# Gathered expert rows in pairs: two rows per VectorE operation, with row sums and scalings on ScalarE

## The chip, the cores and the metric

One core of a Trainium2 chip runs the kernel in one launch. The metric is the device time of that launch in microseconds (us), the median of several executions; lower is better. PE is TensorE (the matmul engine), DVE is VectorE, ACT is ScalarE, POOL is GpSimd and SP is SyncE, which here only issues DMAs.

## The reference, cut to what matters

A decoder layer on 1024 tokens of width 1024. Its first part (a gated MLP beside a state-space model, with projections) is not touched by the change. The second part is a PEER feed-forward layer: each token gets 8 heads x 16 retrieved experts, each expert being one row of a table `u` and one row of a table `v` (16384 rows of 1024 float32 each), and then a last RMS norm:

```
idx, g = top 16 of 256 product-key candidates per head, softmax over them
act = gelu(einsum('thkd,td->thk', u_tab[idx], t))
w   = g * act
y   = einsum('thk,thkd->td', w, v_tab[idx])
x   = x + gt2 * y
return _rmsnorm(x, g_final)
```

For one token that is 128 dot products with rows of `u`, and a sum of 128 rows of `v` with weights.

## The kernel before, in words

The 1024 tokens are 8 blocks of 128, and a token stands on a partition. After about 900 us the scores and choices exist and the feed-forward layer starts, in which the blocks are treated in two ways at the same time.

*Dense blocks.* For five blocks (640 tokens) all 16384 experts are computed by matmul, as 128 tiles `i` of 128 experts. `stage1` (L917 to L931) forms the products `pa` of tile `i` in 2 x 24 matmuls of 128x320, and ACT puts a gelu on each half (L929). `weigh` (L941 to L951) multiplies by the choice weights `Gt` (DVE, L946, two halves), ACT casts the result to the high part `wh` (L949) and DVE forms the low part `wl` (L950). `load_u` and `load_v` (L902 to L915) fetch a tile's tables on SP's queue, ACT casts the high part (L905, L913), DVE the low part (L906, L914). After every four tiles (a group, 32 in all) `stage2` (L955 to L1006) multiplies by the rows of `v` in 10 units of 12 matmuls of 128x512: two blocks add up in PSUM (`res`, L964), for three blocks the result `pd` (L973) is added to `acc` by DVE (L981). `load_g` (L933 to L939) fetches the weights `Gt` of a group as two tiles in three buffers, by DMAs issued on ACT's queue.

*Gathered blocks.* For the other three blocks only the chosen rows are fetched. The generator `side_work` (L858 to L890) does it row by row. For each of 128 rows of `u`: POOL issues an indirect DMA of 128x1024 float32 into a slot `ru` of a ring of 6 (tag "row", 4 KB a partition each, L871), and one DVE instruction multiplies it with the block's tokens `hn` and adds up along the row into a column of `act` (L874, followed by a small instruction that reads the accumulator). Then gelu and the weights, and for each of 128 rows of `v` another gather into the ring (`rv`, L882) and one DVE instruction `gacc = rv * act + gacc` (L887; L885 for the first). At the end `finish` (L830 to L844) multiplies by `gt2` (L834), adds `x1` (`xf`, loaded by a DMA on POOL's queue, L850), takes the RMS norm (L836 on ACT, small operations of DVE, L843) and stores. The two constant rows `gt2` and `g_final` are fetched once for the whole loop into tiles of their own (`final_rows`, L853 to L856).

The main loop (end of the listing) goes through the 128 tiles and after each pulls six rows of the side work. A scheduler then sets one static order per engine; each engine takes its instructions strictly in that order. At the end the remaining side work is pulled (`pull(10 ** 9)`), and the last `stage2` finishes the five dense blocks: it loads `x1` on POOL's queue, multiplies `acc` by `gt2` (L999) and adds (L1000), and each finished `pd` or `res` goes through L834, L835, L836 and L843 of `finish`.

## Time and profile before

| | us |
|---|---|
| median of 3 executions | 2688.28 |
| the three | 2693.47, 2676.6, 2688.28 |
| span of the profiled execution | 2681.3 |
| the part ahead of the loop (not touched) | about 913 |
| loop with the side work, 913 to about 2622 | about 1709 |
| from the last `pa` matmul to the end | about 59 |

The profile is of one execution, and its engine times are shares of its span of 2681.3 us, which lies 7.0 us under the median and inside the three executions. A busy share is an average over the whole span; what matters for a change in the loop is read from the loop's own stretches, and there from who waits for whom. "Idle before" is time an engine stood before an instruction, with the instruction or DMA that ended the wait.

### The profile page before, as it was taken

What the parts mean: (1) busy time and instruction counts of PE and PEld (TensorE: products, weight loads), DVE (VectorE), ACT (ScalarE), POOL (GpSimd) and SP (SyncE); (2) the same over time, 40 slices, a digit from 0 to 9 for tenths busy, and PEclk for the clock granted to TensorE, in tenths of its full rate; (3) what the DMA queues carried; (4) which work ended last, traced back from release to release, by engine and by line L of the source; (5) the groups of instructions that cost most, each with busy time, mean ns of one, the idle gap of its engine ahead of it and who ended that gap; (6) DMA issues with size and microseconds to landing.
All of it is one profiled execution on the core that took longest, in us unless ns stands there. A gap on an engine that the chain in (4) does not pass through costs nothing.

```text
span 2681.3 us, 39165 instructions
## 1 busy us (share of the span) xinstructions
PE 2549.5 (95%) x14119; PEld 2171.5 (81%) x14119; DVE 2302.3 (86%) x5013; ACT 903.2 (34%) x1612; POOL 1038.4 (39%) x842
## 2 busy tenths in 40 slices
PE   6999999999878999999999999999999999999995
PEld 2557676588667898999889999888998899998894
DVE  7984699869899888888898988789897889888998
ACT  2311246578877422222222222222222222222222
POOL 0001000000000255566665665556565456555662
PEclk9996999999997999999999999999999999999998
DMA  9646232342545699999999999989999899998995
GB/s 351 114 151 181 101 134 103 111 157 111 200 139 198 236 348 316 324 330 330 330 359 342 344 332 324 331 312 345 335 341 333 301 330 368 336 332 305 353 322 201
DMA packets 298115, 724.76 MB, mean 270 GB/s; under 512 B 42384, under 2 KB 133008, under 8 KB 292384
## 3 DMA queue, kind: packets, MB, share of 16 engines
q0 software_dynamic: 112832, 411.09, 41.9%
q1 hardware_dynamic: 88800, 254.48, 26.6%
q10 hardware_dynamic: 96288, 56.69, 7.5%
q8 instruction: 111, 1.82, 0.3%
q14 instruction: 84, 0.69, 0.1%
HBM read 658.60 MB, written 62.39 MB: 269 GB/s over the span
## 4 chain that ended last, share of the span: by engine, by line
PE 24%; issue 23%; DVE 21%; POOL 15%; DMA 10%; ACT 5%; POOLq 0%; ACTq 0%; DVEq 0%
POOL rv L882 12%; PE pa L927 6%; DVE jk L874 4%; DMA Gt<-G_d 4%; PE pd L973 4%; POOL ru L871 3%; ACT b L687 3%; PE res L964 3%; PE pq L724 2%; PE po L626 2%; PE pgs L689 2%; DMA ru<-in_peer_u_dram,ix 1%; ACT GS L692 1%; PE pzs L360 1%; DMA vr<-in_peer_v_dram 1%
## 5 line engine op out<-in xcount | busy, mean ns | idle before, releaser
L927 PE MATMUL pa<-Th,u 128*128 128x320 f32 x4096 | 912.4, 310 | 8.7 <-DVE acc L981 5.3
L871 POOL DMA_INDIRECT ru<-in_peer_u_dram,ix x384 | 503.2, 1310 | 1016.4 <-issue 702.0
L927 PEld LDWEIGHTS pa<-Th,u 128*128 128x128 f32 x4096 | 688.3, 188 | 13.5 <-issue 3.3
L882 POOL DMA_INDIRECT rv<-in_peer_v_dram,ix x384 | 515.0, 1341 | 341.7 <-DVE gacc L887 271.1
L927 PE MATMUL pa<-Tl,u 128*128 128x320 f32 x2048 | 634.3, 310 | 0.0
L973 PE MATMUL pd<-v,wh 128*128 128x512 f32 x1536 | 482.4, 392 | 17.0 <-ACT v L913 6.9
L887 DVE SCALAR_TENSOR_TENSOR gacc<-rv,act,gacc 128x1024 f32<-128x1024 f32 x381 | 487.7, 1280 | 8.0 <-DMA rv<-in_peer_v_dram,ix 5.1
L874 DVE CUSTOM_DVE_ANT_0 jk<-ru,hn 128x1024 bf16<-128x1024 f32 x384 | 468.0, 1219 | 14.0 <-DMA ru<-in_peer_u_dram,ix 10.8
L927 PEld LDWEIGHTS pa<-Tl,u 128*128 128x128 f32 x2048 | 385.8, 188 | 1.2
L973 PEld LDWEIGHTS pd<-v,wh 128*128 128x128 f32 x1536 | 288.3, 189 | 81.8 <-ACT v L913 10.7
L964 PE MATMUL res<-v,wh 128*128 128x512 f32 x1024 | 319.4, 390 | 0.8 <-ACT wh L949 0.8
L973 PE MATMUL pd<-v,wl 128*128 128x512 f32 x768 | 299.9, 391 | 0.2 <-DVE wl L950 0.2
L946 DVE TENSOR_TENSOR w<-w,Gt 128x320 f32<-128x320 f32 x256 | 123.6, 483 | 184.7 <-DMA Gt<-G_d 181.4
L905 ACT CAST u<-ur 128x1024 fp32r<-128x1024 f32 x128 | 134.4, 1050 | 429.2 <-PE pd L973 231.1
L949 ACT CAST wh<-w 128x640 fp32r<-128x640 f32 x128 | 93.1, 728 | 492.7 <-DVE w L946 492.4
L687 ACT ACTIVATE b<-hot,gT 128x128 f32<-128x128 f16 x520 | 233.0, 536 | 59.5 <-PE pgs L689 40.2
L689 PE MATMUL pgs<-a,b 128*128 128x128 f32 x1280 | 191.0, 302 | 43.3 <-DVE a L679 21.0
L689 PEld LDWEIGHTS pgs<-a,b 128*128 128x128 f32 x1280 | 172.5, 210 | 65.2 <-ACT b L687 32.7
L964 PEld LDWEIGHTS res<-v,wh 128*128 128x128 f32 x1024 | 192.1, 188 | 40.7 <-ACT wh L949 1.2
L929 ACT ACTIVATE w<-pa 128x320 f32<-128x320 f32 x256 | 109.5, 434 | 281.5 <-PE pa L927 228.3
L964 PE MATMUL res<-v,wl 128*128 128x512 f32 x512 | 199.2, 390 | 1.4 <-DVE wl L950 1.4
L973 PEld LDWEIGHTS pd<-v,wl 128*128 128x128 f32 x768 | 144.8, 188 | 31.0 <-DVE wl L950 0.6
(348 smaller groups left out, 2994.5 us busy)
## 6 DMA issues: line engine op xcount, KB each, us to landing
vr<-in_peer_v_dram SPq DMA_DIRECT2D x128, 512.0 KB, 7.1
ur<-in_peer_ut_dram SPq DMA_DIRECT2D x128, 512.0 KB, 7.1
G_d<-GS SPq DMA_DIRECT2D x40, 1024.0 KB, 5.9
Gt<-G_d ACTq DMA_DIRECT2D x64, 640.0 KB, 16.4
wada<-in_w_ada_dram SPq DMA_DIRECT2D x17, 1024.0 KB, 13.3
wo<-in_w_out_dram SPq DMA_DIRECT2D x8, 1024.0 KB, 4.9
ru<-in_peer_u_dram,ix POOLq DMA_INDIRECT x384, 7.2
rv<-in_peer_v_dram,ix POOLq DMA_INDIRECT x384, 7.3
```

The costliest lines, as they stand in the source:

```text
L687: A.activation(b1[:, n], hot[:, :, o + n], AF.Copy, scale=gT[:, s1 + o + n:s1 + o + n + 1])
L689: T.matmul(pg[:, o // 4, (o % 4) * P:(o % 4 + 1) * P], b1[:, o % 2], a1[:, o % 4], start=True, stop=True)
L871: G.indirect_dma_start(out=row, out_offset=None, in_=a["peer_u"], in_offset=bass.IndirectOffsetOnAxis(ap=ix[:, s:s + 1], axis=0))
L874: V.tensor_tensor_reduce(out=junk, in0=row, in1=hn, scale=1.0, scalar=0.0, op0=ALU.mult, op1=ALU.add, accum_out=act[:, s:s + 1])
L882: G.indirect_dma_start(out=row, out_offset=None, in_=a["peer_v"], in_offset=bass.IndirectOffsetOnAxis(ap=ix[:, s:s + 1], axis=0))
L887: V.scalar_tensor_tensor(ac, row, act[:, s:s + 1], ac, op0=ALU.mult, op1=ALU.add)
L905: A.copy(u[:, 0], ur)
L927: T.matmul(pa[:, :NN], l[:, k, :], r[:, k, ns], start=(k == 0 and m == 0), stop=(k == KD - 1 and m == 2))
L929: A.activation(w[:, ns], pa[:, :NN], AF.Gelu_apprx_tanh)
L946: V.tensor_mul(w3, w3, Gt[i // QG][n][:, :, q * 32:(q + 1) * 32])
L964: T.matmul(res[tb][:, n, :], l[:, ts], r[:, n * 512:(n + 1) * 512], start=(g == 0 and q == 0 and m == 0), stop=(g == NGR - 1 and q == QG - ...
L973: T.matmul(po, l[:, ts], r[:, n * 512:(n + 1) * 512], start=(q == 0 and m == 0), stop=(q == QG - 1 and m == 2))
```

## The change

The gathered rows are handled in pairs (`GP = 2`). A ring slot holds two rows, and there are 4 slots (8 rows, 8 KB a partition and slot) in place of 6 of one row. `fetch` issues the two gathers of a pair one behind the other.

For `u`, DVE multiplies the pair in place by the tokens in one plain multiplication of 128x2048, and ACT sums each row by an activation with `accum_out`. For `v`, ACT scales each row in place by its weight (the first pair into the sum), and DVE adds the pair to a sum of two rows in one addition of 128x2048; at the block's end the two halves of the sum are added. The rows `gt2` and `g_final` are no longer kept: each block fetches them at its end into a slot of the ring, by two DMAs on ACT's queue; the `x1` tile takes a ring slot too, as it did before. The order of pulls is the same (six rows per tile), and ahead of the loop each engine's order is the same as before.

```
-            for s in range(NS):
-                row = rp.tile([P, D], F32, tag="row", name=f"ru{n}_{s}")
-                G.indirect_dma_start(out=row, ...)
-                junk = rp.tile([P, D], BF16, tag="junk", name=f"jk{n}_{s}", bufs=1)
-                V.tensor_tensor_reduce(out=junk, in0=row, in1=hn, scale=1.0, scalar=0.0, op0=ALU.mult,
-                                       op1=ALU.add, accum_out=act[:, s:s + 1])
-                yield
+            def fetch(src, s0, name):
+                row = rp.tile([P, GP, D], F32, tag="row", name=f"{name}{n}_{s0}")
+                for e in range(GP):
+                    G.indirect_dma_start(out=row[:, e], out_offset=None, in_=a[src],
+                                         in_offset=bass.IndirectOffsetOnAxis(ap=ix[:, s0 + e:s0 + e + 1], axis=0))
+                return row
+
+            for s in range(0, NS, GP):
+                row = fetch("peer_u", s, "ru")
+                V.tensor_mul(row, row, bcast(hn, 1, GP))
+                for e in range(GP):
+                    A.activation(junk, row[:, e], AF.Copy, accum_out=act[:, s + e:s + e + 1])
+                    yield
...
-                    V.scalar_tensor_tensor(ac, row, act[:, s:s + 1], ac, op0=ALU.mult, op1=ALU.add)
...
+            ac2 = rp.tile([P, GP, D], F32, tag="hn", name=f"gacc{n}", bufs=1)
+            for s in range(0, NS, GP):
+                row = fetch("peer_v", s, "rv")
+                for e in range(GP):
+                    A.activation(row[:, e] if s else ac2[:, e], row[:, e], AF.Copy, scale=act[:, s + e:s + e + 1])
+                    yield
+                if s:
+                    V.tensor_add(ac2, ac2, row)
+            ac = ac2[:, 0]
+            V.tensor_add(ac, ac, ac2[:, 1])
+            final_rows(rp, n)
+            x1 = load_x1(NDB + n, rp.tile([P, GP, D], F32, tag="row", name=f"xf{n}")[:, 0])
```

The static order changes only in the loop. DVE near the end, before: the weights of the last two tiles (`w`, `wl`), with the rows `rv_113` and later of the last gathered block between and behind them (line numbers of the kernel before).

```order
L950 TENSOR_TENSOR wl_22826<-w_22770,wh_22825 128x640
L946 TENSOR_TENSOR w_22852<-w_22852,Gt_0_22518 128x320
L887 SCALAR_TENSOR_TENSOR gacc_20995<-rv_116_22982,act_18351,gacc_20995 128x1024
L946 TENSOR_TENSOR w_22852<-w_22852,Gt_1_22520 128x320
L950 TENSOR_TENSOR wl_22908<-w_22852,wh_22907 128x640
L887 SCALAR_TENSOR_TENSOR gacc_20995<-rv_119_22991,act_18351,gacc_20995 128x1024
L834 TENSOR_TENSOR res_7531<-res_7531,fin_7698 128x512
L834 TENSOR_TENSOR pd_2_0_23160<-pd_2_0_23160,fin_7698 128x512
L1000 TENSOR_TENSOR x_1_23043<-x_1_23043,acc 128x1024
L887 SCALAR_TENSOR_TENSOR gacc_20995<-rv_127_23015,act_18351,gacc_20995 128x1024
L834 TENSOR_TENSOR pd_2_1_23173<-pd_2_1_23173,fin_7698 128x512
L1000 TENSOR_TENSOR x_1_23043<-x_1_23043,acc 128x1024
```

DVE near the end in the changed kernel, from the last additions of pairs (`rv_126` is the last pair; L894 there is the addition, L896 that of the halves, L955 and L959 what L946 and L950 were, L1008 what L999 was).

```order
L894 TENSOR_TENSOR gacc_20616<-gacc_20616,rv_124_22626 128x2048
L990 TENSOR_TENSOR acc<-acc,pd_4_1_22283 128x512
L915 TENSOR_TENSOR u_22357<-ur_22355,u_22357 128x1024
L894 TENSOR_TENSOR gacc_20616<-gacc_20616,rv_126_22632 128x2048
L1008 TENSOR_TENSOR acc<-acc,fin_22639 128x1024 x3
L955 TENSOR_TENSOR w_22302<-w_22302,Gt_0_22137 128x320
L896 TENSOR_TENSOR gacc_20616<-gacc_20616 128x1024
L955 TENSOR_TENSOR w_22302<-w_22302,Gt_1_22139 128x320
L835 TENSOR_TENSOR gacc_20616<-gacc_20616,fin_22639 128x1024
L959 TENSOR_TENSOR wl_22363<-w_22302,wh_22362 128x640
L836 TENSOR_TENSOR xf_22642<-xf_22642,gacc_20616 128x1024
```

The last gathered row thus moves from behind the last tile's weights, among the final multiplications, to ahead of the weights of the third tile from the end, and its `finish` stands among the last tiles.

ACT's queue around the issue of a group's second `Gt` tile, before (L929 the gelus, L949 `wh`, L938 the issue).

```order
L929 ACTIVATE w_10925<-pa_0_10926 128x320
L938 DMA Gt_1_11072<-G_d 128x10x128
L929 ACTIVATE w_10925<-pa_1_10952 128x320
L905 CAST u_10980<-ur_10978 128x1024
L949 CAST wh_10985<-w_10925 128x640
L938 DMA Gt_0_11554<-G_d 128x10x128
L929 ACTIVATE w_11012<-pa_0_11013 128x320
L913 CAST v_10991<-vr_10989 128x1024
L929 ACTIVATE w_11012<-pa_1_11039 128x320
L949 CAST wh_11076<-w_11012 128x640
```

The same place of the changed kernel, in a stretch where rows of `v` are scaled (L891; L938 are the gelus there, L947 the issue, L958 `wh`).

```order
L938 ACTIVATE w_11276<-pa_0_11277 128x320
L891 ACTIVATE rv_58_11358<-rv_58_11358,act_7700 128x1024
L938 ACTIVATE w_11276<-pa_1_11303 128x320
L891 ACTIVATE rv_60_11432<-rv_60_11432,act_7700 128x1024
L947 DMA Gt_1_11423<-G_d 128x10x128
L891 ACTIVATE rv_60_11432<-rv_60_11432,act_7700 128x1024
L958 CAST wh_11336<-w_11276 128x640
L947 DMA Gt_0_11905<-G_d 128x10x128
L891 ACTIVATE rv_62_11438<-rv_62_11438,act_7700 128x1024
L938 ACTIVATE w_11363<-pa_0_11364 128x320
L891 ACTIVATE rv_62_11438<-rv_62_11438,act_7700 128x1024
```

The issue of `Gt_1` now stands behind the second gelu and two rows' scalings, where it stood right behind the first gelu.

## Rows read from the trace of the kernel before

**Rows 1.** Windows of the loop (913 to 1531 and 1531 to 2601 us) and of the end; the columns are the stretch, its length, the busy time of PE, PEld, DVE, ACT and POOL with their instructions, the granted clock of PE as a share of full speed, the DMA share and GB/s.

```profile
913.00:1531.00 618.00, 614.51 (x3449) 560.08 (x3448) 539.15 (x718) 159.23 (x228) 370.21 (x278) 1.00 0.94 337
1531.00:2601.00 1070.00, 1058.28 (x5928) 962.85 (x5927) 930.11 (x1226) 265.49 (x385) 625.73 (x476) 1.00 0.92 332
...
2640.00:2681.30 41.30, 15.58 (x56) 11.95 (x54) 36.20 (x117) 8.05 (x22) 1.79 (x4) 0.73 0.46 178
```

**Rows 2.** The chain of waits in the loop: start, length and what, for the first pieces of three groups.

```profile
916.48 28.16 PE pa L927 x192
...
1475.64 28.16 PE pa L927 x192
...
1531.02 7.05 PE pa L927 x48
```

**Rows 3.** PE's timeline: the first matmul of the last group's `pa`, and the last `stage2` (start, length, form, idle before).

```profile
2601.40 0.31 PE L927 MATMUL pa<-Th,u 128*128 128x320 f32 x1
...
2622.51 0.63 PE L964 MATMUL res<-v,wh 128*128 128x512 f32 x2
...
2624.81 1.19 PE L964 MATMUL res<-v,wh 128*128 128x512 f32 x4 [0.75 <-ACT wh L949]
2627.38 0.74 PE L964 MATMUL res<-v,wl 128*128 128x512 f32 x2 [1.38 <-DVE wl L950]
...
2653.11 1.22 PE L973 MATMUL pd<-v,wh 128*128 128x512 f32 x2 [5.95 <-DVE x L835]
...
2661.14 0.39 PE L973 MATMUL pd<-v,wl 128*128 128x512 f32 x1
```

**Rows 4.** Groups of DVE's instructions by form, 1200 to 2600 us: count, busy us, mean ns of one, idle before.

```profile
L887 DVE SCALAR_TENSOR_TENSOR gacc<-rv,act,gacc 128x1024 f32<-128x1024 f32 x359 | 459.5, 1280 | 6.5 <-DMA rv<-in_peer_v_dram,ix 3.8
L874 DVE CUSTOM_DVE_ANT_0 jk<-ru,hn 128x1024 bf16<-128x1024 f32 x260 | 316.9, 1219 | 6.6 <-DMA ru<-in_peer_u_dram,ix 4.4
L906 DVE TENSOR_TENSOR u<-ur,u 128x1024 fp32r<-128x1024 f32 x100 | 121.7, 1217 | 2.4 <-ACT u L905 2.4
...
L950 DVE TENSOR_TENSOR wl<-w,wh 128x640 fp32r<-128x640 f32 x100 | 81.6, 816 | 0.0
```

**Rows 5.** Groups of ACT's instructions by form, whole span.

```profile
L905 ACT CAST u<-ur 128x1024 fp32r<-128x1024 f32 x128 | 134.4, 1050 | 429.2 <-PE pd L973 231.1 <-DMA ur<-in_peer_ut_dram 197.6 <-issue 0.2
L346 ACT ACTIVATE hT<-hT,mod,G 128x512 f32<-128x512 f32 x8 | 6.1, 807 | 5.2 <-DVE G L323 4.3 <-DVE hT L286 0.8
L836 ACT ACTIVATE sqf<-xf 128x1024 bf16<-128x1024 f32 x3 | 3.2, 1055 | 30.4 <-DVE xf L835 30.4
L836 ACT ACTIVATION_READ_ACCUMULATOR sqf<-xf 128x1 f32 x3 | 0.6, 188 | 0.0
```

**Rows 6.** The timelines of DVE (first two) and POOL (last three) from 2618 to 2625 us.

```profile
2618.19 0.82 DVE L950 TENSOR_TENSOR wl<-w,wh 128x640 fp32r<-128x640 f32 x1
2619.32 2.60 DVE L887 SCALAR_TENSOR_TENSOR gacc<-rv,act,gacc 128x1024 f32<-128x1024 f32 x2
2618.54 1.28 POOL L882 DMA_INDIRECT rv<-in_peer_v_dram,ix  x1 [2.15 <-DVE gacc L887]
2620.87 1.86 POOL L882 DMA_INDIRECT rv<-in_peer_v_dram,ix  x1 [1.06 <-DVE gacc L887]
2623.04 0.94 POOL L882 DMA_INDIRECT rv<-in_peer_v_dram,ix  x1 [0.31 <-issue]
```

**Rows 7.** The page, the group of the gathers of `v` on POOL (busy us, mean ns), and its DMA issues with the median time to landing (KB each, us).

```profile
L882 POOL DMA_INDIRECT rv<-in_peer_v_dram,ix x384 | 515.0, 1341 | 341.7 <-DVE gacc L887 271.1
...
Gt<-G_d ACTq DMA_DIRECT2D x64, 640.0 KB, 16.4
...
rv<-in_peer_v_dram,ix POOLq DMA_INDIRECT x384, 7.3
```

**Rows 8.** Timelines around a wait for `Gt`: four instructions of DVE, then one of ACT.

```profile
2408.03 1.28 DVE L887 SCALAR_TENSOR_TENSOR gacc<-rv,act,gacc 128x1024 f32<-128x1024 f32 x1
2418.04 0.49 DVE L946 TENSOR_TENSOR w<-w,Gt 128x320 f32<-128x320 f32 x1 [8.73 <-DMA Gt<-G_d]
2458.41 0.48 DVE L946 TENSOR_TENSOR w<-w,Gt 128x320 f32<-128x320 f32 x1
2474.10 0.49 DVE L946 TENSOR_TENSOR w<-w,Gt 128x320 f32<-128x320 f32 x1 [7.82 <-DMA Gt<-G_d]
2418.56 0.73 ACT L949 CAST wh<-w 128x640 fp32r<-128x640 f32 x1 [13.14 <-DVE w L946]
```

**Rows 9.** Who waits for whom, 1531 to 2601 us: total us, times, longest.

```profile
DVE w L946 <- DMA Gt<-G_d: 127.1, 19, 9.4
DVE jk L874 <- DMA ru<-in_peer_u_dram,ix: 4.4, 9, 0.8
```

**Rows 10.** Timelines of DVE in a `finish` inside the loop (the first two rows: its first and last small operation's neighbours) and at the end, and of SP's queue at the end (last row).

```profile
1494.78 0.15 DVE L140 TENSOR_SCALAR msf<-msf 128x1 f32<-128x1 f32 x1 [0.30 <-ACT sqf L836]
...
1498.42 1.29 DVE L843 SCALAR_TENSOR_TENSOR xf<-xf,rf,fin 128x1024 f32<-128x1024 f32 x1
...
2648.32 1.28 DVE L887 SCALAR_TENSOR_TENSOR gacc<-rv,act,gacc 128x1024 f32<-128x1024 f32 x1
2675.30 2.74 DVE L843 SCALAR_TENSOR_TENSOR x<-x,rf,fin 128x512 f32<-128x512 f32 x4
2669.74 8.66 SPq L844 DMA_DIRECT2D out_dram<-x  x10
```

28 lines of the change are left out of this document (9 added, 19 removed).

## The prediction

> **What bounds the kernel now.** I read the windows first. In both stretches of the loop PE is busy for all but 3.5 of 618 us and 11.7 of 1070 us [rows 1]; DVE is at 87% (930.11 of 1070), POOL at 58%, ACT at only 25%. Then the chain of waits, for a group's length: 192 matmuls of `pa` take 28.16 us [rows 2], and the 120 of `stage2`, at the 0.227 us a step that the last group shows when nothing stalls, 27.2; together 55.38. From 916.48 to 1531.02 [rows 2] are eleven groups, 614.54 us against 609.2 at that pace; from there to 2601.40 [rows 3] nineteen, 1070.4 against 1052.2. So in thirty groups PE lost only 5.4 + 18.2 = 23.6 us. That is the first fact: no relief of DVE can give more than about 24 us in the loop.
>
> Third, who nearly ties with PE. DVE runs without a gap except at one place per group, where the first multiplication by the next `Gt` waits for its DMA: 127.1 us in 19 waits [rows 9]. Two such waits end 56.06 us apart [rows 8], PE's period. The rows themselves are hardly waited for: 4.4 us for `ru` [rows 9].
>
> Last the end. The last `pa` matmul ends at about 2622.5; the last `stage2` then takes 39.0 us to 2661.5 where 27.2 would do. It waits twice for the last weights (0.75 and 1.38) and once 5.95 us for a PSUM bank that DVE's finishing has not freed [rows 3], and the matmuls behind that stop run at the lower clock: granted 0.73 on average from 2640 on, against 1.00 in the loop [rows 1]. DVE is late there since the last rows of the gathered block, up to `rv_127` at 2648.32, stand in its queue among the finishing operations [rows 10].
>
> **The change part by part.** *DVE.* Removed are 2 x 384 single-row operations of 1.22 and 1.28 us [rows 4]; consecutive ones overlap, so a row costs a step of about 1.14 to 1.20. Added are 384 operations of 128x2048, which no row shows. From plain multiplications or additions of 640 and 1024 columns, 0.816 and 1.217 us [rows 4], the slope is 1.04 ns a column, and 2048 columns come to 2.29 us, a step of 2.2. If the cost were halved (two columns at a time) it would be about 1.2, if nothing overlapped 2 x 1.22 = 2.44. I take 2.2, by the slope: 0.1 to 0.2 us less per pair, 54 to 77 us of DVE in all, some 2 us per group. In itself that is worth nothing, since DVE waits in every group; what it moves is the circle below.
>
> *ACT.* Added are 768 operations. A summed row is like the row of squares: 1.055 plus 0.188 for reading the sum [rows 5]; overlapped, 1.18. A scaled row lies between the plain cast of that size, 1.050, and that plus two pointer operands (the 512-column row with two takes 0.807, twice that for 1024 would be 1.61) [rows 5]; I take 1.15, near the cast. That is 384 x 1.18 + 384 x 1.15 = 895 us beside its 425 in the loop: from 25% to about 77%. It is cover, not path, as long as `wh` and the gelus are not held long: one row's work ahead of each, 1.2 us, sometimes two.
>
> *`Gt`.* A group's second `Gt` tile needs the buffer that DVE's last multiplication by the older tile frees; then ACT's queue issues the DMA, and DVE waits for it, in a circle. From the waiting multiplication at 2418.04 to the freeing one at 2458.41 are 40.4 us of DVE without a gap [rows 8]; a landing takes 16.4 [rows 7]; together 56.8, against 56.06 seen and PE's 55.38. So this circle, not PE alone, costs the loop's lost microseconds. In the changed order of DVE I counted the same stretch, each operation by its step above: 36.8 us on average over the groups, 33 to 43 in single ones, since fewer rows' work stands in it. That makes 53.2. But the issue now stands behind a gelu and up to two scalings more in ACT's queue: 2 to 5 us. The circle is then 55 to 58 us; with 3 us it is 56.2, 0.15 more than now, some +5 us over thirty groups. The bounds are -20 (PE alone) and 2 x 30 = +60.
>
> *The ring.* Before, a slot's cycle is 0.30 to issue, 7.3 to land [rows 7] and 1.2 for DVE: 8.8 us of the 13.3 that six slots give at 25 rows per group (2.216 us a row). Now a slot holds two rows: two gathers, about 3.7 us, landing 7.7, DVE 2.3, two rows on ACT 2.4: 14.4 to 14.7 us, of 8 x 2.216 = 17.7. Three us are left for waits, but a pair now passes through two in-order queues.
>
> *A gather against DVE.* A gather on POOL that overlaps a DVE operation with two inputs ends about 0.8 us after it: DVE's `wl` ends at 2619.01, the gather at 2619.82; DVE's pair of rows at 2621.92, the gather at 2622.73; with DVE idle it took 0.94 us, against a mean of 1.34 [rows 6, 7]. Behind a 2.2 us operation the mean wait grows by about half of the added 1.1 us, so I use 1.7 us per gather above; 25 gathers x 0.4 = 10 us more per group fit into POOL's 42% of idle time, 23 us. The Trainium skill ("SBUF — State Buffer", Terms) says that DVE and GpSimd share a port pair locked for a whole instruction, and that the loser fully blocks; the rows agree in kind. By that rule alone a gather could cost up to 2.3 + 0.81 = 3.1 us, which would take the slack of three us.
>
> *End of a block.* `gt2` and `g_final` now come by two DMAs per block into a slot, and with the `x1` tile hold two of four slots. Before, there is a pause there as well; I price it at nothing to 5 us, twice, hidden under PE's groups, since the side work runs ahead of need.
>
> *The end.* By DVE's order the last pair now stands ahead of the weights of the third tile from the end, not behind the last. DVE is then free during the last `stage2`, and the 5.95 us stop and the lower clock go: 2622.5 + 2.1 (the two early waits stay) + 27.2 = 2651.8. After the last matmul come 0.7 + 0.7 on DVE, a square and its read of 0.8, some small operations, 3.6 us of the root (1494.78 to 1498.42), two halves of L843 (1.4 of the 2.74) and the store, 3.3 (2678.0 to 2681.3) [rows 10]: 10.7, giving 2662.5 where 2681.3 stood. That is -19 us, with bounds 0 and -24.
>
> Sum against the profiled span: 2681.3 + 5 - 19 = 2667. The median lies 7 us above the span, so 2674 for the measured time. 1%, about what a measurement of this kernel tells from no change, is 27 us: bounds 2661 and 2715.
>
> **The rivals.** *Slower: the ring starves DVE.* Place: the four slots. If the waits in the two queues average over the three us of slack, the rows come late, DVE stands in order behind them, then `w` and `wl`, then PE. With 3.7 us of waits a slot takes 18.4 us, 4.60 per pair instead of 4.43: 0.17 more, 67 us over 384 pairs; less the end's 19, about 2736. It decides when the cycle passes 17.7 us. For it: ACT stands 13.14 us behind `Gt` in each group [rows 8], and now rows' sums and scalings stand behind that too. Against: the side work may catch up in the rest of the group, as before.
>
> *Faster: the relief of DVE counts.* The 23.6 us lost in the loop shrink to a few: -20 and -19, about 2649. For it: the circle of `Gt` gets 3.6 us shorter on DVE. Against: its issue is later. It needs an added delay of under 2 us.
>
> *Nothing at the end.* The loop is as before and the last rows still come late, because the ring runs behind: 2688.
>
> **How the numbers follow.** Forecast 35%, own range 2655 to 2690; slower 27%, faster 22%, nothing 16%. Faster by over 1%: the faster case and a third of the forecast, 0.34. Slower by over 1%: 0.27. Within: 0.39. The range goes from 2648 (the faster case) to 2735 (the slower one's centre): about 2 in 10 lie outside, nearly all above.
>
> **What would show it.** Right: DVE's pairs at 2.2 to 2.3 us; ACT at 75 to 80% of the loop; the PE period still near 55.4 to 56; no stop of 6 us in the last `stage2`, and its matmuls at full clock; the last `rv` before 2622. The slower case: waits of DVE for `ru`, `rv` or ACT's scalings of tens of us, gathers of over 2 us, a period of 57 us or more. The forecast is wrong if ACT's rows cost well over 1.2 us, or if a pair on DVE costs under 2.0 or over 2.4.

## The result, and the profile after

The changed kernel takes 2702.22 us (median) where the kernel before, run on the same chip, takes 2691.95: the ratio is 1.0051, with a 95% interval of 1.0029 to 1.0072. It is slower by 0.5%, and the forecast had been 0.5% faster. The ratio leaves out two of the 20 executions after, which were in a slower state of the chip, and it is not the quotient of the two medians (1.0038).

The profiled execution after has a span of 2710.2 us, 28.9 more than before. Its own run took 2712.0, about 10 us over the median, where the span of before lies about 10 under the median of before. So the ratio, not the two spans, gives the size.

PE's timeline of the kernel after: the first and the last `pa` matmul, the longest stop in the loop, and the start and the end of the last `stage2` (start, length, form; in brackets the idle time before it and what ended it).

```profile
917.78 0.30 PE L936 MATMUL pa<-Th,u 128*128 128x320 f32 x1
...
2570.96 0.80 PE L982 MATMUL pd<-v,wh 128*128 128x512 f32 x1 [6.98 <-ACT v L922]
...
2666.40 0.31 PE L936 MATMUL pa<-Th,u 128*128 128x320 f32 x1
2666.55 0.63 PE L973 MATMUL res<-v,wh 128*128 128x512 f32 x2
2695.98 0.39 PE L982 MATMUL pd<-v,wl 128*128 128x512 f32 x1
```

The loop, from the first to the last `pa`, takes 1748.6 us; before it took 1706.1 (916.3 to 2622.4). From there to the end of the span it is 43.8 us in place of 58.9: the last `stage2` runs in 29.6 without the stop of 5.95 in [rows 3]. So +42.5 in the loop, -15.1 at the end, and 1.5 from the start make the 28.9. By the ratio the whole is about 14 us, and the loop thus some 29.

Where PE loses the 42.5 us can be read from the two traces. In the loop after, PE stands 45.3 us between matmuls (gaps of over 0.15 us), where it stood 15.0. And its granted clock is at 0.5, the lower level of 1.2 GHz, in six stretches of 30.7 us together, each at a stop of 2.1 to 7.0 us; before there is one such stretch of 3.4 us, at a stop of 2.9. Half of PE's busy time in these stretches, an estimate of what the clock costs, is 12.1 us against 1.4. The two differences, 30.3 and 10.7, make up 41.0 of the 42.5. So a stop of PE can cost more here than its own length.

The windows of the loop and of the end, after (columns as in [rows 1]).

```profile
913.00:1531.00 618.00, 598.74 (x3353) 544.82 (x3352) 502.17 (x422) 431.35 (x620) 439.55 (x272) 0.99 0.92 326
1531.00:2601.00 1070.00, 1045.65 (x5811) 948.95 (x5810) 891.52 (x741) 768.84 (x1104) 787.05 (x478) 0.99 0.94 333
...
2667.00:2710.20 43.20, 27.23 (x119) 21.88 (x117) 36.20 (x119) 12.07 (x28) 1.05 (x2) 0.89 0.30 110
```

PE stands 19.3 of 618 and 24.4 of 1070 us, where it stood 3.5 and 11.7 [rows 1]. DVE's share fell from 87% to 83%, and ACT's rose from 25% to 72%. At the end the granted clock is 0.89 in place of 0.73, but both stretches take in time in which PE has no work left. From the last `pa` to the last matmul it is 1.00 after (2667.0 to 2696.4 us) and was 0.91 before (2622.7 to 2661.5).

The page after, groups of the row work (POOL's gathers, ACT's rows, DVE's pairs).

```profile
L875 POOL DMA_INDIRECT ru<-in_peer_u_dram,ix x384 | 634.9, 1653 | 913.0 <-issue 738.5
L875 POOL DMA_INDIRECT rv<-in_peer_v_dram,ix x384 | 628.9, 1638 | 202.2 <-issue 109.9
L891 ACT ACTIVATE rv<-rv,act 128x1024 f32<-128x1024 f32 x378 | 425.8, 1147 | 163.9 <-DMA rv<-in_peer_v_dram,ix 154.9
L883 ACT ACTIVATE jk<-ru 128x1024 bf16<-128x1024 f32 x384 | 405.4, 1056 | 192.5 <-issue 150.9
L881 DVE TENSOR_TENSOR ru<-ru,hn 128x2048 f32<-128x2048 f32 x192 | 438.3, 2287 | 96.7 <-DMA ru<-in_peer_u_dram,ix 84.2
L894 DVE TENSOR_TENSOR gacc<-gacc,rv 128x2048 f32<-128x2048 f32 x189 | 432.5, 2288 | 83.5 <-ACT rv L891 65.6
```

The prices came out nearly as forecast; what is new is the right-hand end of the last two lines. Who DVE waits for, 917 to 2667 us of the kernel after (total us, times, longest):

```profile
DVE ru L881 <- DMA ru<-in_peer_u_dram,ix: 84.2, 54, 4.3
DVE gacc L894 <- ACT rv L891: 65.6, 49, 4.8
DVE w L955 <- DMA Gt<-G_d: 51.5, 14, 9.7
```

Before, DVE's one large wait was for `Gt` [rows 9]. Now it waits 150 us for rows, and for `Gt` only 51.5: in 14 of the 27 groups 4 to 30 (counted from 0), DVE comes to the first multiplication by the second `Gt` tile with no wait for the tile left, and in three more with one of at most 0.9 us. Before, no wait was left in 2 of the 27. In such groups the circle of `Gt` no longer sets the pace: the tile is there before DVE's own queue, with the waits in it, comes to it.

### The profile page after: what moved, and what is told of

Its sections match the earlier page's. It is cut to its first block, busy times and chain, and to the rows that moved or that the text cites. A ratio compares the mean times of both kernels' runs of the same rounds, so it can differ in the third digit from the quotient of the medians.

```text
span 2710.2 us, 39378 instructions
## 1 busy us (share of the span) xinstructions
PE 2554.9 (94%) x14119; PEld 2174.0 (80%) x14119; DVE 2250.2 (83%) x4245; ACT 1717.7 (63%) x2764; POOL 1283.9 (47%) x842
## 4 chain that ended last, share of the span: by engine, by line
DVE 25%; DMA 20%; PE 17%; POOL 15%; issue 14%; ACT 7%; DVEq 0%; ACTq 0%; POOLq 0%
POOL rv L875 13%; DMA ru<-in_peer_u_dram,ix 9%; DMA Gt<-G_d 5%; DVE ru L881 4%; DMA rv<-in_peer_v_dram,ix 4%; PE pa L936 3%; ACT b L688 3%; PE pd L982 3%; PE res L973 2%; PE pq L725 2%; PE po L627 2%; POOL ru L875 1%; DVE a L680 1%; PE pzs L361 1%; DVE gacc L894 1%
## 5 line engine op out<-in xcount | busy, mean ns | idle before, releaser
L875 POOL DMA_INDIRECT ru<-in_peer_u_dram,ix x384 | 634.9, 1653 | 913.0 <-issue 738.5
L936 PE MATMUL pa<-Th,u 128*128 128x320 f32 x4096 | 913.3, 310 | 14.4 <-ACT w L938 6.6
L875 POOL DMA_INDIRECT rv<-in_peer_v_dram,ix x384 | 628.9, 1638 | 202.2 <-issue 109.9
L891 ACT ACTIVATE rv<-rv,act 128x1024 f32<-128x1024 f32 x378 | 425.8, 1147 | 163.9 <-DMA rv<-in_peer_v_dram,ix 154.9
L883 ACT ACTIVATE jk<-ru 128x1024 bf16<-128x1024 f32 x384 | 405.4, 1056 | 192.5 <-issue 150.9
L982 PE MATMUL pd<-v,wh 128*128 128x512 f32 x1536 | 489.2, 395 | 36.7 <-ACT v L922 27.6
L881 DVE TENSOR_TENSOR ru<-ru,hn 128x2048 f32<-128x2048 f32 x192 | 438.3, 2287 | 96.7 <-DMA ru<-in_peer_u_dram,ix 84.2
L894 DVE TENSOR_TENSOR gacc<-gacc,rv 128x2048 f32<-128x2048 f32 x189 | 432.5, 2288 | 83.5 <-ACT rv L891 65.6
L973 PE MATMUL res<-v,wh 128*128 128x512 f32 x1024 | 325.6, 392 | 2.1 <-ACT wh L958 2.1
L688 ACT ACTIVATE b<-hot,gT 128x128 f32<-128x128 f16 x520 | 234.2, 546 | 56.2 <-PE pgs L690 34.6
L915 DVE TENSOR_TENSOR u<-ur,u 128x1024 fp32r<-128x1024 f32 x128 | 156.1, 1220 | 27.2 <-ACT u L914 26.5
L955 DVE TENSOR_TENSOR w<-w,Gt 128x320 f32<-128x320 f32 x256 | 122.4, 484 | 62.5 <-DMA Gt<-G_d 51.5
```

Of the source, the lines that this page charges most:

```text
L688: A.activation(b1[:, n], hot[:, :, o + n], AF.Copy, scale=gT[:, s1 + o + n:s1 + o + n + 1])
L875: G.indirect_dma_start(out=row[:, e], out_offset=None, in_=a[src], in_offset=bass.IndirectOffsetOnAxis(ap=ix[:, s0 + e:s0 + e + 1], axis=0))
L881: V.tensor_mul(row, row, bcast(hn, 1, GP))
L883: A.activation(junk, row[:, e], AF.Copy, accum_out=act[:, s + e:s + e + 1])
L891: A.activation(row[:, e] if s else ac2[:, e], row[:, e], AF.Copy, scale=act[:, s + e:s + e + 1])
L894: V.tensor_add(ac2, ac2, row)
```

## The experiments

Two readings go with each. The *ratio* to the kernel before has an interval of 0.2 to 0.45% to either side (6 to 12 us). *Loop by ratio* is the loop's change against before: (ratio - 1) x 2690, less the change of the end (last `pa` to end of span, from the profile, against 58.9). It is safer than one profile's loop, since two executions with nearly the same loop order (before_rot and before_rot2 below) differ by 12.5 us.

| kernel | ratio, 95% | loop in the profile | last `pa` to end | loop by ratio |
|---|---|---|---|---|
| before | 1 | 1706.1 | 58.9 | 0 |
| after | 1.0051 (1.0029 to 1.0072) | 1748.6 | 43.8 | +29 |
| act64 | 1.0008 (0.9974 to 1.0041) | 1736.1 | 43.8 | +17 |
| actconst | 1.0046 (1.0011 to 1.0080) | 1742.4 | 43.8 | +27 |
| dvehalf | 0.9925 (0.9895 to 0.9955) | 1713.9 | 41.4 | -3 |
| split | 1.0107 (1.0062 to 1.0152) | 1752.9 | 48.4 | +39 |
| oldops | 1.0053 (1.0022 to 1.0084) | 1747.4 | 41.4 | +32 |
| hoistv | 1.0089 (1.0052 to 1.0125) | 1752.4 | 43.6 | +39 |
| oldops_hoist | 0.9998 (0.9973 to 1.0022) | 1727.1 | 43.7 | +15 |
| pairs_old | 1.0253 (1.0209 to 1.0297) | 1775.2 | 70.3 | +57 |
| pairs_rot | 1.0162 (1.0126 to 1.0198) | 1767.7 | 61.5 | +41 |
| before_rot | 0.9976 (0.9946 to 1.0006) | 1696.9 | 58.8 | -6 |
| before_rot2 | 0.9925 (0.9899 to 0.9951) | 1709.4 | 53.6 | -15 |
| before_uneven | 0.9933 (0.9905 to 0.9962) | 1684.5 | 61.2 | -20 |
| before_rot2_un | 0.9892 (0.9854 to 0.9930) | 1693.9 | 54.7 | -25 |

In every kernel of the table the profile's loop, less PE's gaps and less half of PE's busy time at the lower clock, comes to 1684 to 1692 us (before 1689.6, after 1691.2). What tells the loops apart is thus how long PE stands, and the clock with it; the experiments ask what makes it stand.

### Four kernels whose order was made anew

*noact* leaves ScalarE's row work out, but for the first instructions of a block:

```
-                    A.activation(junk, row[:, e], AF.Copy, accum_out=act[:, s + e:s + e + 1])
+                    if s == 0 and e == 0:
+                        A.activation(act, row[:, 0, :NS], AF.Copy)
...
-                    A.activation(row[:, e] if s else ac2[:, e], row[:, e], AF.Copy, scale=act[:, s + e:s + e + 1])
+                    if s == 0:
+                        A.activation(ac2[:, e], row[:, e], AF.Copy, scale=act[:, s + e:s + e + 1])
```

> The changed kernel without ScalarE's work on the rows: the sums of the u pairs and the scalings of all but the first v pair are left out (one small copy per block keeps the weights defined), so DVE's pair operations, gathers and the ring of four slots stay. Theory Q (what the change loses in the loop, about 40 us of the profiled execution, comes through ScalarE's queue: casts, wh and the Gt issue stand behind rows): the loop is back at or below its time before and the earlier end of the side work stays, ratio to before 0.980 to 0.992. Theory P (gathers slowed by DVE's 2.3 us operations make rows late whatever ScalarE does): DVE still waits over 60 us for ru and rv, ratio 1.00 to 1.01.

*actfree* keeps these instructions on ScalarE, but they read another tile and write `junk`, so that they wait for no row and no row waits for them:

```
-                    A.activation(junk, row[:, e], AF.Copy, accum_out=act[:, s + e:s + e + 1])
+                    A.activation(junk.rearrange("p (a b) -> p a b", a=2), Tl[:, 0:2, 0:512].bitcast(F32), AF.Copy,
+                                 accum_out=act[:, s + e:s + e + 1])
...
```

> The changed kernel with the same amount of work on ScalarE, 762 operations of 1024 columns, which read a constant tile and write a scratch tile in place of the gathered rows (the sums and the scaled rows are not used). ScalarE's queue is as full as in the changed kernel, but it never waits for a gather and holds no ring slot. Theory Q in the form 'full queue' (the volume alone holds back casts and Gt): still slower, ratio 1.002 to 1.010. Theory Q in the form 'waiting queue' (ScalarE stands in order for rows that have not landed, 146 us for rv, and the casts stand behind that): ratio 0.980 to 0.993, PE's waits for the casts of v under 8 us where they were 26.

*gt_sp* issues the `Gt` loads from SP's queue:

```
-            nc.scalar.dma_start(t, G_d[n * nb:(n + 1) * nb, :, g * QG:(g + 1) * QG, :].rearrange("b j i t -> j b (i t)"))
+            nc.sync.dma_start(t, G_d[n * nb:(n + 1) * nb, :, g * QG:(g + 1) * QG, :].rearrange("b j i t -> j b (i t)"))
```

> The changed kernel with the Gt DMAs issued on SyncE's queue and not on ScalarE's. Theory G (the second Gt tile is late because its issue stands behind rows on ScalarE, and everything follows from that): waits for Gt shrink and the ratio to before falls to 0.985 to 0.995. Theory Q without G (rows hold back casts and wh themselves): ratio 1.00 to 1.01, as the changed kernel, PE's waits for v's casts stay above 20 us.

*singles9* handles single rows in nine slots with the new split of the work (two of the slots take the rows of the last norm, and the addition of the halves goes):

```
-GP = 2
+GP = 1
-... rows=4 ...
+... rows=9 ...
-                V.tensor_mul(row, row, bcast(hn, 1, GP))
+                V.tensor_mul(row[:, 0], row[:, 0], hn)
...
```

> The changed kernel's division of labour (DVE multiplies or adds, ScalarE sums or scales) with single rows: DVE operations of 128x1024, a ring of nine one-row slots, the last-norm rows in two of them at each block's end. A slot's cycle by the same working is 11.5 us of 9 x 2.2 = 19.9, so 8 us of slack where pairs had 3; gathers stand behind 1.2 us operations again (1.33 us each where pairs have 1.65). If late rows are the cause (ring of pairs, theory R, or theory P): ratio 0.983 to 0.995. If the volume on ScalarE is the cause (Q, full queue): 1.003 to 1.015.

Measured: noact 1.0244 (1.0194 to 1.0293), actfree 1.0653 (1.0598 to 1.0708), gt_sp 1.0130 (1.0081 to 1.0179), singles9 1.0705 (1.0650 to 1.0760). All are slower than the changed kernel, even the one with ScalarE's row work left out, whose loop took 1790.6 us. Less work and a longer loop: what these runs share is that the scheduler made a new static order for each, so none tells of its edit alone. They were inconclusive on the theories and pointed to the order as a cause. One thing their traces share: most of PE's stops in the loop end with a cast of a `v` tile (67.8 of 71.4 us in noact, 150.1 of 157.4 in actfree, 34.8 of 60.7 in gt_sp, 148.6 of 181.3 in singles9). A section below comes to these casts.

From here on, the order of every engine is written out instruction by instruction (as dependences of issue order without semaphores), so that only what the text names differs. No run has the written-out order with nothing changed. The nearest to it is actconst, whose trace has the instructions of PE, DVE and POOL and SP's transfers in the order of the kernel after, one by one, and whose ratio is 1.0046.

### One engine's time, in the changed kernel's order

*act64*: ScalarE's rows only 64 columns long. *actconst*: ScalarE's rows full length, but reading another tile, as in actfree. *dvehalf*: DVE's pairs half as long.

```
-                    A.activation(junk, row[:, e], AF.Copy, accum_out=act[:, s + e:s + e + 1])
+                    A.activation(junk[:, :64], row[:, e, :64], AF.Copy, accum_out=act[:, s + e:s + e + 1])
...
-                V.tensor_mul(row, row, bcast(hn, 1, GP))
+                V.tensor_mul(row[:, :, :512], row[:, :, :512], bcast(hn[:, :512], 1, GP))
...
-                    V.tensor_add(ac2, ac2, row)
+                    V.tensor_add(ac2[:, :, :512], ac2[:, :, :512], row[:, :, :512])
```

> The changed kernel with every engine's order written out as it stands there, so that nothing moves; only ScalarE's operations on the rows are cut to 64 of 1024 columns (the other columns are neither summed nor scaled), some 0.3 us in place of 1.15 to 1.2. DVE's pairs, the gathers and the waits stay. Theory V (ScalarE's time on the path of a row, as volume or as latency, makes the loop 40 us longer in the profile): the loop falls to about 1710 us (1749 in the changed kernel, 1706 before), ratio to before 0.982 to 0.990. Theory P (gathers and DVE's long operations make the rows late): loop 1730 to 1750, DVE still waits over 80 us for ru and rv, ratio 0.997 to 1.006.

> The changed kernel, every engine's order as it stands there; ScalarE does all of its 768 operations at full size, but all except the first pair of a block read a constant tile and write a scratch tile, so that the rows' sums and scalings are not used. ScalarE's queue is as full as in the changed kernel, without waits for gathers, and a slot goes from DVE straight to the next gather. Theory V as volume: the loop stays at 1735 to 1755 us, ratio 1.000 to 1.008. Theory V as latency (two queues in a row's path): loop about 1710 us, ratio 0.982 to 0.992. Theory P: like the changed kernel.

> The changed kernel, every engine's order as it stands there; DVE's pair operations run over 512 of 1024 columns of each row (the rest is neither multiplied nor added), 1.22 us in place of 2.29, ScalarE as in the changed kernel. Theory P: gathers go back to 1.3 us, the waits for rows fall, loop about 1710 us, ratio 0.982 to 0.990. Theory V: DVE has 11 us per group more, but ScalarE still holds slots and casts: PE's stalls fall by half at most, loop 1725 to 1740, ratio 0.990 to 0.999.

Measured: 1.0008, 1.0046 and 0.9925. Three quarters of ScalarE's row time taken away (from 831 to 225 us) is worth about 12 us of loop, hardly more than the intervals; freeing its rows from the gathers is worth nothing that can be told. Half of DVE's row time is worth some 32 us, which brings the loop back to that of before (the ratio is in theory V's range, the profile's loop near theory P's). So in this order DVE's time weighs most, in spite of its 83%. The gathers follow it: with DVE's operations half as long they fall from 1653 to 1157 ns (dvehalf, the page):

```profile
L875 POOL DMA_INDIRECT ru<-in_peer_u_dram,ix x384 | 444.3, 1157 | 1068.7 <-DMA vr<-in_peer_v_dram 655.6
L875 POOL DMA_INDIRECT rv<-in_peer_v_dram,ix x384 | 447.6, 1166 | 379.5 <-DVE gacc L894 265.8
```

That gain is of shorter work on DVE and shorter gathers together; the next run parts them.

### Split: the pairs as two operations

```
-                V.tensor_mul(row, row, bcast(hn, 1, GP))
+                for e in range(GP):
+                    V.tensor_mul(row[:, e], row[:, e], hn)
...
-                    V.tensor_add(ac2, ac2, row)
+                    for e in range(GP):
+                        V.tensor_add(ac2[:, e], ac2[:, e], row[:, e])
```

> The changed kernel, every engine's order as it stands there, with one thing undone: each DVE operation on a pair (128x2048, 2.29 us) is two operations of 128x1024 one behind the other, which together take DVE as long (2 steps of 1.14). ScalarE, ring and gathers stay. Theory L (the length of DVE's single operation: a gather on POOL waits for the running one to end, so 1.65 us where 1.33 stood, which leaves POOL almost no pace to catch up after a stop): gathers 1.30 to 1.40 us, loop 1710 to 1725 us, ratio to before 0.990 to 0.998. Theory D (DVE's busy time as such, which the halved operations took away): nothing changes, gathers may be shorter but ratio 1.003 to 1.008.

Measured: 1.0107. Who DVE waits for in this kernel, and its gathers of `u`, in the columns used above:

```profile
DVE w L957 <- DMA Gt<-G_d: 156.1, 26, 11.4
DVE ru L882 <- DMA ru<-in_peer_u_dram,ix: 17.1, 21, 2.3
```

```profile
L875 POOL DMA_INDIRECT ru<-in_peer_u_dram,ix x384 | 545.7, 1421 | 976.5 <-DMA vr<-in_peer_v_dram 652.4
```

The gathers get 0.23 us shorter and DVE's waits for rows shrink from 84.2 to 17.1 us. The loop gains nothing: the waits for `Gt` are back (156.1). So the long gathers and the waits for rows are real, but shortening them does not bring the time back. Theory L, which forecast a ratio of 0.990 to 0.998, falls; the ratio is a little above theory D's range too.

### The old arithmetic in the new order

*oldops* has the changed kernel's order, ring slots and rows of `gt2` and `g_final` per block, but DVE does each row with the old instruction, at the place where its pair stood:

```
-                V.tensor_mul(row, row, bcast(hn, 1, GP))
...
-                    A.activation(junk, row[:, e], AF.Copy, accum_out=act[:, s + e:s + e + 1])
+                    V.tensor_tensor_reduce(out=junk, in0=row[:, e], in1=hn, scale=1.0, scalar=0.0, op0=ALU.mult,
+                                           op1=ALU.add, accum_out=act[:, s + e:s + e + 1])
...
-                if s:
-                    V.tensor_add(ac2, ac2, row)
+                for e in range(GP):
+                    if s:
+                        V.scalar_tensor_tensor(ac2[:, e], row[:, e], act[:, s + e:s + e + 1], ac2[:, e],
+                                               op0=ALU.mult, op1=ALU.add)
```

> The changed kernel's order on every engine, its ring of four pairs and its last-norm rows per block, with the arithmetic of the kernel before: per row one multiply-and-sum of 128x1024 and one multiply-and-add on DVE, in the places of the pair operations; ScalarE's operations on rows are gone (but for the first pair of a block). Output as the reference. Theory L: gathers 1.35 us, DVE a little busier, loop 1705 to 1720 us as before, the end 15 us shorter as in the changed kernel: ratio 0.990 to 0.997. Theory D and theory O (the order itself is what loses in the loop): loop 1735 to 1755, ratio 1.002 to 1.008.

Measured: 1.0053, the changed kernel's ratio. Its second stretch of the loop and its waits on DVE:

```profile
1531.00:2601.00 1070.00, 1049.75 (x5847) 954.54 (x5846) 930.82 (x1226) 265.55 (x381) 595.54 (x478) 0.99 0.92 333
```

```profile
DVE w L959 <- DMA Gt<-G_d: 167.0, 27, 10.4
...
DVE jk L882 <- DMA ru<-in_peer_u_dram,ix: 3.8, 3, 1.5
```

The busy times of DVE and ACT are those of before to a microsecond (930.82 and 265.55 against 930.11 and 265.49 [rows 1]), and DVE waits for `Gt` and not for rows, as before. Yet PE is busy for 8.5 us less in that stretch, and the loop is about 30 us longer. But for the first pair of a block nothing of the new arithmetic is left in this kernel: the new order loses this much without it. What came with that order is still there, the four slots of pairs and the last-norm rows of each block. DVE waits only 3.8 us for rows of `u` and 0.3 for rows of `v`, so the ring is not seen to hold it, but no run has the new order with six slots of one row.

### The late casts of `v`

In the new order the casts of seven last tiles of a group (39, 43, 75, 79, 83, 119, 123) stand behind the next group's first multiplication by the second `Gt` tile on DVE, and behind the `wh` cast that waits for it on ACT; in the order before none of them does. The last group's, on DVE:

```
+L923 v123<-vr123
 L955 w124<-w124,Gt31_1
 L915 u125<-ur125
 L959 wl124<-w124,wh124
 L894 gacc<-gacc,rv_112
 L894 gacc<-gacc,rv_114
-L923 v123<-vr123
```

`stage2` needs these tiles. In the kernel after, PE's longest stops end with such a cast (the 6.98 us above). Who PE waits for there, 917 to 2667 us, and, as the last row, the largest of these waits in the kernel before, 917 to 2620 us:

```profile
PE pd L982 <- ACT v L922: 26.0, 12, 7.0
PE pa L936 <- ACT w L938: 6.6, 4, 2.6
...
PE pd L973 <- ACT v L913: 5.4, 6, 1.5
```

Of the 45.3 us that PE stands in the loop after, 21.8 end with a cast (on either engine) of one of the seven tiles; before it was 1.1. In oldops it is 22.2 of 42.7. The four kernels whose order was made anew fit this: in noact, actfree, gt_sp and singles9 the last tile's cast on DVE stands behind that wait in 24, 25, 10 and 20 of 30 groups, against 7 in the kernel after. That goes together with their longer loops, but it was not tested in them.

*hoistv* moves six of the seven ahead of the wait on both engines (tile 83's stays where it is: by the program it needs a buffer that PE frees later, and no run tried it); *oldops_hoist* does the same to oldops.

> The changed kernel, every engine's order as it stands there, but for six tiles (39, 43, 75, 79, 119, 123): their cast of v on ScalarE is moved ahead of the next group's first wh, and their low part on DVE ahead of that group's first multiplication by its second Gt tile, which waits for the DMA. Theory H (the changed order put these last tiles of a group behind an instruction that waits for Gt, so that PE stops for v): PE's waits for v fall from 26 to under 10 us, loop 1722 to 1735 us (1749 in the changed kernel), ratio 0.995 to 1.001. Theory K (the circle of Gt is too long in any case, the stops only move): loop 1740 to 1755, ratio 1.003 to 1.008.

> The old arithmetic in the changed kernel's order (1.0053 measured, loop 1747 us, PE waiting 27 us of its 40 us for casts of v tiles on ScalarE and VectorE), with six of the seven casts of v that stand behind the next group's wait for Gt moved ahead of it on both engines. Theory V (the late casts are what the order loses; with the changed arithmetic the same move gave nothing because there VectorE was held by its waits for rows): the loop falls to 1715 to 1725 us, ratio 0.992 to 0.997. Rival G (the circle of the weights Gt, whose landing takes some 3 us longer in this order, is the loss and PE only meets it at the casts): the stops move to other operands, the loop stays at 1740 to 1750, ratio 1.003 to 1.007.

Measured: 1.0089 and 0.9998. With the new arithmetic the move gives nothing: PE's waits for ACT's `v` fall to 13.6 us, but others appear, and PE still stands 44.6 us. With the old arithmetic PE stands 29.9 us in place of 42.7, and the move takes about half of the loss away (1727.1 in place of 1747.4; by ratio +15 in place of +32), between the two forecasts. Of PE's stops left in oldops_hoist, 9.2 us are at tile 83, the one not moved (its casts, the 84th of each engine, end at 2037.5 on ACT and 2045.9 on DVE):

```profile
2037.54 0.50 PE L986 MATMUL pd<-v,wh 128*128 128x512 f32 x1 [2.97 <-ACT v L926]
...
2045.95 0.79 PE L986 MATMUL pd<-v,wh 128*128 128x512 f32 x1 [6.24 <-DVE v L927]
```

So with the old arithmetic the late casts account for some 17 us that were tested (give or take 11, by the two intervals) and up to 9 that were not. The rest of the 32 us is within what two such readings differ by. For the kernel after, with the new arithmetic, it is not shown what its loss would be without them. The rival, a later landing of `Gt`, is there in the traces, but it does not explain what the move gave: where DVE waits for the second tile, the multiplication starts on average 17.0 us after the issue in oldops and 17.9 in oldops_hoist, against 15.7 before.

### The new arithmetic in the old order, and the old order rearranged

*before_rot* moves, in 26 groups, two rows on DVE into its wait for `Gt`, and brings the last block's rows forward; nothing else moves:

```
 L946 w48<-w48,Gt12_0
 L874 jk1_1<-ru1_1
+L874 jk1_2<-ru1_2
+L874 jk1_3<-ru1_3
 L946 w48<-w48,Gt12_1
```

> The kernel before, every engine's order as it stands there, but on DVE the next two rows are moved ahead of the multiplication that waits for a group's second Gt tile (26 groups), so that they are worked off during that wait and not in the circle from that multiplication to the one that frees the next buffer; in the last gathered block the rows behind close up, which ends the side work some ten rows earlier. Output as the reference. Theory K (the circle, 41.2 + 15.2 us, sets the period): 2.4 us less in the circle, period at PE's 55.4 to 55.7, loop 1690 to 1698 us in place of 1706, and 8 to 15 us less at the end: ratio 0.988 to 0.993. If the circle is not what sets the period: only the end, 0.994 to 0.998.

*pairs_old* has the changed kernel's instructions in the order of before (a pair where its second row stood; ScalarE's sums 2.2 us behind the product and its scalings 3.5 us ahead of the addition, by the times of the old trace), and *pairs_rot* the same in the order of before_rot.

> The changed kernel's instructions (pairs on DVE, sums and scalings on ScalarE, ring of four pairs, last-norm rows per block) in the order of the kernel before: every instruction that both kernels have stands where it stood there, each pair operation in the place of its second row, ScalarE's operations on rows where their times in the trace before put them (sums behind the product, scalings 3.5 us ahead of the addition); the last norms behind the last rows. Output as the reference. With the run of the old arithmetic in the new order (1.0053, loop 1747 us) this closes a table of two by two. Theory O (the order that the framework made for the new durations loses the 40 us in the loop): loop 1700 to 1718 us, ratio 0.992 to 1.000. Theory A (the pairs themselves cost it, through gathers of 1.65 us and two queues): loop 1730 to 1755, ratio 1.001 to 1.010.

> As the run beside it, on the order of the kernel before with two rows moved into each wait for Gt and the last rows earlier (0.9976 with the old arithmetic, loop 1697 us). Theory O: loop 1688 to 1705 us, and the side work ends some ten rows earlier, ratio 0.985 to 0.994, faster than both kernels. Theory A: loop 1725 to 1750, ratio 1.000 to 1.008.

Measured: 0.9976, 1.0253 and 1.0162. DVE's waits in pairs_old, 917 to 2660 us:

```profile
DVE gacc L894 <- ACT rv L891: 76.4, 39, 5.5
DVE ru L881 <- DMA ru<-in_peer_u_dram,ix: 75.0, 44, 5.3
DVE w L955 <- DMA Gt<-G_d: 72.5, 12, 11.1
DVE wl L959 <- ACT wh L958: 44.7, 42, 2.7
```

In before_rot the profile's loop is as theory K had it (1696.9 us), but the end did not get shorter (58.8): PE stands 4.5 us for `wh` there. The ratio's interval (0.9946 to 1.0006) leaves room for no gain at all. The two kernels with pairs are slower than both of their theories forecast.

With the four corners at hand (all but the first with the ring of pairs), loop by ratio: old order and old arithmetic 0; old order and new arithmetic +57; new order and old arithmetic +32; new and new +29. The arithmetic costs much in the order made for the old one, and nothing that can be told in the order that was made for it; but that order loses some 30 us whichever arithmetic it has. One caution: ScalarE's places in pairs_old follow my rule, and another rule may do better.

### Two rearrangements tested for their own sake

*before_rot2* is before_rot with the end rearranged: the last two tiles' weights ahead of the last seven rows on DVE, and the gathered block's last products and the `x1` additions in the gap ahead of the first `res`.

```
 L946 w127<-w127,Gt31_0
 L946 w127<-w127,Gt31_1
 L950 wl127<-w127,wh127
+L887 gacc<-rv_121
...
+L887 gacc<-rv_127
+L834 gacc<-gacc,fin0
 L834 res0<-res0,fin0
```

> The kernel before with two rows in each wait for Gt (as before_rot) and with a new order of DVE at the end: the weights of the last two tiles stand ahead of the last seven rows, and the products of the gathered block and the x1 additions stand in the gap before the first res product. Output as the reference. Theory: loop about 1697 us as in before_rot, the wait of 4.5 us for wh in the last stage2 goes, and DVE has 6 us less to do behind the last matmul: from the last pa to the end 48 to 53 us where it was 59, ratio to before 0.989 to 0.995, below both kernels. Rival: the end is set by the chain of small operations of the last norms, not by DVE's volume; then it stays at 56 to 59 and the ratio at 0.997.

Measured: 0.9925. The last `pa` to the last matmul is 33.3 us in place of 38.9, and the whole end 53.6, just over the forecast. PE's wait for `wh` did not go (4.2 us); the stop of 5.95 us did. So a third of the 15.1 us that the change gains at the end needs none of its arithmetic, and oldops shows the whole of it without. The profile's loop, 1709.4, is not the 1697 of the forecast; by the ratio it is 15 us shorter than before.

*before_uneven* tests whether the new order loses because rows are spread unevenly (DVE's busy time between the two multiplications that bound the circle is 34.6 to 49.6 us in oldops, 38.6 to 42.5 before). In the order of before, nine pairs of neighbouring groups have three rows moved from the first group's circle to the second's.

```
 L946 w49<-w49,Gt12_0
 L874 jk1_18<-ru1_18
-L874 jk1_19<-ru1_19
 L946 w49<-w49,Gt12_1
+L874 jk1_19<-ru1_19
```

> The kernel before, every engine's order as it stands there, but in nine pairs of neighbouring groups three rows on DVE are taken out of the first group's stretch (from the multiplication that waits for the second Gt tile to the one that frees the next buffer) and put into the second group's. Nothing is added or left out; the stretch is 3.6 us shorter in nine groups and 3.6 longer in nine others, as uneven there as in the changed kernel's order. Output as the reference. Theory U (per group the longer of PE's 55.4 and the circle counts, so the short ones give nothing back): -1.0 and +3.6 us per pair of groups, 9 x 2.6 = 23 us, ratio 1.006 to 1.010. Rival (only the sum of DVE's work counts, a late group is made up in the next): ratio 0.998 to 1.003.

Measured: 0.9933, with busy times from 36.1 to 46.0 us: the theory fell. PE runs through, and the windows show it:

```profile
913.00:1531.00 618.00, 617.27 (x3476) 563.93 (x3475) 541.44 (x722) 159.04 (x229) 363.86 (x278) 1.00 0.94 338
1531.00:2601.00 1070.00, 1069.99 (x6046) 979.90 (x6044) 949.64 (x1241) 272.20 (x389) 635.85 (x483) 1.00 0.93 336
```

*before_rot2_un* has both rearrangements.

> The kernel before, with the two changes of order of before_rot2 (two rows into each wait for Gt; at the end the last tiles' weights ahead of the last rows) and with that of before_uneven (in nine pairs of neighbouring groups three rows moved from the first to the second). Theory A (the gains have separate places: the rows' spread takes PE's stops in the loop away, loop near 1685 to 1690 us, and the end is 33 us to the last matmul): ratio 0.986 to 0.990. Rival S (PE's stops in the loop vary from execution to execution and the loop of before_uneven was a good one, or rows in the wait and uneven rows take the same slack): ratio 0.991 to 0.995.

Measured: 0.9892 (0.9854 to 0.9930), 2661.22 us beside 2688.19: the fastest version found, with the arithmetic of before. Why three rows later in every other group make PE's stops go was not settled: the sum of DVE's work is the same, and its waits for `Gt` fall from 180.3 us in 27 (before) to 123.9 in 19 (before_uneven, both 917 to 2660 us):

```profile
DVE w L946 <- DMA Gt<-G_d: 180.3, 27, 9.4
...
DVE w L946 <- DMA Gt<-G_d: 123.9, 19, 9.0
```

## Why the prediction was wrong

*Prices: right.* A pair on DVE 2.29 us (forecast 2.29), a scaled row 1.147 (1.15), a summed row 1.056 and its read (1.18), a gather 1.65 and 1.64 (1.7), ACT 72% of the loop (75 to 80, so a little under). The gather's price is partly luck: by its own working, half of an added 1.1 us on a mean of 1.34, it would be 1.9; the mean grew by 0.3 us where the operation grew by 1.0.

*The end: right, a little large.* -15.1 in place of -19: the last `stage2` took 29.6 us against 29.3 forecast, and what follows the last matmul 13.8 in place of 10.7. That the two early waits stay was luck: one of another length came in their place (2.14 us, as long as the two together). oldops has the same short end with the old arithmetic, so it came from the order, as the prediction had it. The clock of 0.73 that the prediction read from 2640 on takes in 19.8 us behind the last matmul; up to that one, at 2661.5, it was 0.84.

*The circle of `Gt`: the step that failed.* "+5 us over thirty groups" was about +29 by the ratio and +42.5 in the profile. The prediction took this circle for the group's period and put it at 56.2 us. Measured from one group's first multiplication by its second `Gt` tile to the next group's (27 groups), the period is 57.4 us; the same reading gives 56.4 before. Of the terms, the stretch was forecast at 36.8 us of DVE; its busy time was 37.3, but it holds 5.9 us of idle time on average, 4.2 of it waits at the additions and products of pairs. The prediction left these to the ring ("Three us are left for waits") and put them at nothing in the circle. The issue's delay was forecast at 2 to 5 us and was 0.25. So the stretch was 6.4 us too short and the delay some 3 us too long, and the circle itself was no longer the period: in 14 of 27 groups no wait for `Gt` ends it. The ring's slack was shaky besides: its terms as listed (3.7, 7.7, 2.3 and 2.4) add up to 16.1 us, which leaves 1.6 of 17.7; the 14.4 to 14.7 comes out only if the landing takes in the second gather, which the text does not say.

*The cause behind it.* The prediction took the new static order as neutral but for the counted stretch. oldops shows that this order, with its ring, has the loss without the new arithmetic, and oldops_hoist that about half of it is then the late casts of `v`, which were readable in the order beforehand: no term of the sum asked where they went. In the kernel after itself 21.8 of PE's 45.3 us of stops end with these casts, but moving six of them brought nothing (hoistv), so how its loss divides between them and DVE's waits for rows is argued and not shown.

*The slower rival* named a real thing (150 us of waits for rows), and by the prediction's own signs (such waits, a period of 57 us or more) it was nearer than the forecast. But the waits are not what decides: in split most of them go, in oldops nearly all, and the loop stays as long. Two limits lie close together, DVE's queue with its row waits and the order's waits at `Gt` and `v`; taking one away shows the other. This is a reading of these runs; none takes both away at once. The relief of DVE paid only when it was large (dvehalf).

*What stays open:* what in the order, beside the casts, loses the rest; why moving the casts brings nothing with the new arithmetic; whether the new arithmetic could gain in an order made by hand for it; and the gain of before_uneven.

## What to carry to other kernels

Where a scheduler makes one static order, a change of arithmetic is two changes: test the old arithmetic in the new order and the new one in the old order before giving either the credit. When two engines are tied within a few per cent, look through the new order for producers (here casts) that have moved behind a wait of their queue, and add the waits inside a counted stretch to it, not only its busy time.

## What the runs showed of the hardware

A gather's time on POOL depends on the DVE operation that is under way when it starts. On average it is 1.31 and 1.34 us with single rows before, 1.65 behind pairs, 1.41 behind split pairs and 1.16 behind half pairs. The gathers of `u` before:

```profile
L871 POOL DMA_INDIRECT ru<-in_peer_u_dram,ix x384 | 503.2, 1310 | 1016.4 <-issue 702.0
```

In the kernel after, DVE's operations and the gathers that overlap them (two timelines):

```profile
2550.93 2.29 DVE L894 TENSOR_TENSOR gacc<-gacc,rv 128x2048 f32<-128x2048 f32 x1
2553.15 0.82 DVE L959 TENSOR_TENSOR wl<-w,wh 128x640 fp32r<-128x640 f32 x1
2553.88 0.48 DVE L955 TENSOR_TENSOR w<-w,Gt 128x320 f32<-128x320 f32 x1
```

```profile
2551.55 2.48 POOL L875 DMA_INDIRECT rv<-in_peer_v_dram,ix  x1 [0.30 <-issue]
2554.34 0.94 POOL L875 DMA_INDIRECT rv<-in_peer_v_dram,ix  x1 [0.31 <-issue]
```

The first gather ends at 2554.03, 0.81 us behind the end of the addition (2553.22) that was under way when it started; the `wl` that follows the addition on DVE does not hold it further. The next starts 0.02 us ahead of the end of `w` (2554.36) and takes 0.94. Of the 768 gathers of this trace, 164 start with no operation under way on DVE and 29 while DVE only adds a `pd` from PSUM to `acc`: all but one of these take about 0.94 us. Of the other 575, 568 end, to within 0.06 us, 0.81 us behind the operation under way, or take 0.94 where that is longer. The longest but one takes 3.04 us. The extra time is thus the rest of the operation that is under way when the gather starts, and half pairs make gathers short in part because 293 of them start with DVE idle (40 before).

Larger than any of this is the order: reordering DVE's instructions alone, with every instruction the same, moved this kernel from 1 to 0.9892.
